# Ten of 22 gate/up pairs of a feed-forward stage as seven half-block products on normalised x

## The chip, the cores and the metric

One core of one Trainium2 chip runs the whole program in one launch. The metric is device microseconds (us) of one execution, and lower is better. TensorE (PE) multiplies a 128x128 weight block (loaded first, by PEld in the profile) with a moving tile of up to 512 columns and adds the result up in PSUM. VectorE (DVE), ScalarE (ACT) and GpSimd (POOL) work on tiles of 128 partitions. SyncE (SP) issues nearly all DMA transfers.

## The reference

Two layers over 512 tokens of width 1024. The four SwiGLU stages, two in each layer, are where the change lies:

```python
def rmsnorm(x, g):
    xf = x.astype(jnp.float32)
    y = xf * lax.rsqrt(jnp.mean(xf * xf, axis=-1, keepdims=True) + RMS_EPS)
    return (y * g.astype(jnp.float32)).astype(x.dtype)

def swiglu(x, w_gate, w_up, w_down):          # 1024 -> 2816 -> 1024
    return (jax.nn.silu(x @ w_gate) * (x @ w_up)) @ w_down

for i in range(DEPTH):                        # DEPTH = 2
    h = h + 0.5 * swiglu(rmsnorm(h, norm_ffn1[i]), ...)
    h = h + mixer_i(rmsnorm(h, norm_mix[i]))  # attention, differs by layer
    h = h + 0.5 * swiglu(rmsnorm(h, norm_ffn2[i]), ...)
    gate = jax.nn.sigmoid(rmsnorm(h, norm_ple[i]) @ w_ple_gate[i])
    h = h + gate * (p[i] @ w_ple_proj[i])
```

All of it is float32. The input embedding p is what "the 256 KB loads of p" below refers to.

## The kernel before, in words

Everything is kept transposed: the feature axis on the partitions, the 512 tokens along the free axis. `h` is eight tiles (chunks) of 128x512.

**Exact products from rounded parts.** PE reads a rounded float32 format (fp32r). Each operand is therefore split in two: `hi`, its rounded copy (ACT, L121), and `lo`, what is left over (DVE, L122: source minus `hi`). `mm3` (L139) then issues three matmuls for each 128x128 weight block: hi·hi, hi·lo and lo·hi (L142 to L144). A *unit* (L129) is 1024 columns of weights: a DMA of 512 KB on SP's queue (L135) into a `wr` tile, then ACT's rounding into `wh` and DVE's low part into `wl`. `mm_unit` multiplies the eight blocks of a unit with the eight chunks of x: 24 matmuls 512 columns wide.

**A feed-forward stage** (`ffn`) has 22 gate/up pairs of 128 hidden features each, then eight output chunks of the down projection. A pair is two units, gate into a bank of PSUM tag `mm`, up into one of tag `sc`, so 48 matmuls. The moving operand is `xg`: h times the gain, split, but not yet divided by the root mean square. That factor, the row `R` (128x512, the same on all partitions), is only known when h is complete and squared, so it is put on afterwards: DVE multiplies the gate bank by R (L236), ACT takes the silu (L237), DVE multiplies the up bank by R (L238), POOL multiplies both (L239), and the product is split for the down projection by ACT and DVE. The 22 products stay in 44 tiles of the pool `act`.

**What sets the order.** The program is written as such a sequence; a scheduler of the framework puts each engine's instructions in a fixed order by the order in which they were written and by when its simulation finds them ready. Code inside `tc.high_priority()` is put ahead. Pools give the buffers: 3 `wr`, 4 `wh`, 4 `wl`, 59 `act`, 8 `tmp`; PSUM banks 3 `mm`, 2 `sc`, 2 `tr`, 1 `ob`. A DMA into a `wr` tile waits until the unit before it in that buffer has been read by ACT and DVE. Each engine, and each DMA queue, takes its instructions strictly in that order. Before the second to fourth feed-forward stages, `rcol` and `R` are made while the first pairs already run on PE; in the first stage the squares are made after the first pair.

**Other stages.** The mixers and the embedding step use the same units. In the V projection of the mixer (L322 to L324) the moving operand is a 256-column slice of the weights, so its matmuls are 256 wide, each with a weight load of its own.

Of the kernel before, what the change touches and what calls it, by code (L numbers as in the profile page):

```python
# [36 lines left out]
class Trunk:
# [52 lines left out]
    def setup(self):  # L90
# [21 lines left out]
        for c in range(KC):  # L112
            self.h[c] = self.hp.tile([P, T], F32, tag="h", name=self.nm("h"))
            nc.sync.dma_start(self.h[c], io["xT"][:, c, :])
            self.norm_split(c)
            if c in (0, 2):
                self.ahead.append(self.unit(io["gu1"][0, 0, c // 2]))
# [99 lines left out]

    def ffn(self, i, which, k_next):
        nc, io = self.nc, self.io
        gu, dn = io[f"gu{which}"], io[f"dn{which}"]  # L220
        xg, a = self.xg, []
        for m in range(NF):
            pgu = []
            for j in range(2):
                u = self.ahead.pop(0) if self.ahead else self.unit(gu[i, m, j])
                p = self.sbank() if j else self.bank()
                self.mm_unit(p, u, xg, True, True)
                pgu.append(p)
                if j == 0 and m == 0 and (i or which == 2):
                    self.rcol  # L230
            if m == 0 and i == 0 and which == 1:
                for c in range(KC):
                    self.norm_square(c)
            R = self.R
            t1, t2 = self.tmp(), self.tmp()
            nc.vector.tensor_tensor(t1, pgu[0], R, op=ALU.mult)  # L236
            nc.scalar.activation(t1, t1, AF.Silu)  # L237
            nc.vector.tensor_tensor(t2, pgu[1], R, op=ALU.mult)  # L238
            nc.gpsimd.tensor_tensor(t2, t1, t2, op=ALU.mult)  # L239
# [822 lines left out]
```

## Time and profile before

| | |
|---|---|
| median of 3 runs | 2126.43 us (2123.27 to 2127.14) |
| the profiled execution | 2126.64 us, of which the span of its instructions 2124.8 us |
| TensorE's granted clock, mean | 1.00 of full speed (0.995) |
| DVE, ACT and POOL busy | 1132.3, 783.8 and 352.3 us |
| POOL's product L239 | 88 instructions, 1309 ns each |
| DMA, mean over the span | 95 GB/s |

How to read it: each engine's busy time is a share of the span, but no stage has the same share. Of interest is the stretch of the pairs, where PE's matmuls follow each other without a gap. Busy time of PE counts matmuls that overlap their neighbours (they are pipelined), so it is the distance between the starts of two matmuls that says what one costs.

### The profile page before, as it was taken

Reading aid. Unit: us, or ns where it says so; the run is one execution under the profiler, and the core shown is the slowest. Engines: PE = TensorE matmul, PEld = TensorE weight load, DVE = VectorE, ACT = ScalarE, POOL = GpSimd, SP = SyncE. Lnnn points to the kernel's source line nnn. Section 1 sums busy time; section 2 is a strip of 40 time slices with the busy share of each in tenths; the row PEclk is TensorE's granted clock in tenths of the full one; section 3 lists DMA queues with packets and bytes.
Section 4 is the critical chain, followed back from the end, with each engine's and each line's share of the span. In section 5 each row is a group of like instructions: output and inputs, shape, how many; then the busy total and the mean of one; then the engine's idle time right before and its main releaser. Section 6 shows DMA issues by size and latency. Waiting matters only on the chain.

```text
span 2124.8 us, 25520 instructions
## 1 busy us (share of the span) xinstructions
PE 2085.4 (98%) x9950; PEld 1734.6 (82%) x9950; DVE 1132.3 (53%) x1793; ACT 783.8 (37%) x1255; POOL 352.3 (17%) x248
## 2 busy tenths in 40 slices
PE   8999999999999999999999999999999999999998
PEld 6888888777787888888888888888888888888886
DVE  6554432699786444543354555333778744553334
ACT  4332222465544333222343233223656533232232
POOL 3111101233211111101111111013222210110111
PEclk9999999999999999999999999999999999999999
DMA  5333333221223233333333322334333223323331
GB/s 171 98 99 99 95 96 98 85 75 56 65 68 92 90 99 99 99 90 96 105 97 99 99 93 93 95 97 124 105 105 102 82 90 99 99 91 96 94 107 60
DMA packets 75385, 202.02 MB, mean 95 GB/s; under 512 B 16896, under 2 KB 24576, under 8 KB 75264
## 3 DMA queue, kind: packets, MB, share of 16 engines
q1 hardware_dynamic: 74976, 200.29, 30.8%
q8 instruction: 78, 1.28, 0.3%
q14 instruction: 43, 0.35, 0.1%
q10 hardware_dynamic: 288, 0.10, 0.0%
HBM read 191.97 MB, written 2.59 MB: 92 GB/s over the span
## 4 chain that ended last, share of the span: by engine, by line
PE 89%; DVE 5%; ACT 2%; issue 1%; POOL 1%; DMA 0%; SPq 0%; DVEq 0%; POOLq 0%; ACTq 0%
PE mm L143 15%; PE mm L144 15%; PE mm L142 15%; PE sc L142 12%; PE sc L143 12%; PE sc L144 12%; PE mm L322 1%; PE mm L323 1%; PE mm L324 1%; PE tr L349 1%; PE ob L359 1%; PE ob L360 1%; PE sc L428 1%; ACT wh L121 1%; DVE act L572 1%
## 5 line engine op out<-in xcount | busy, mean ns | idle before, releaser
L121 ACT ACTIVATE wh<-wr 128x1024 fp32r<-128x1024 f32 (+1 forms) x360 | 374.6, 1042 | 995.0 <-issue 431.1
L122 DVE TENSOR_TENSOR wl<-wr,wh 128x1024 fp32r<-128x1024 f32 (+1 forms) x343 | 510.2, 1488 | 314.1 <-ACT wh L121 313.1
L143 PE MATMUL mm<-act,wh 128*128 128x512 f32 (+1 forms) x1560 | 609.7, 391 | 3.0 <-DVE act L169 2.1
L142 PE MATMUL mm<-act,wh 128*128 128x512 f32 (+1 forms) x1560 | 609.1, 391 | 1.0 <-ACT wh L121 0.6
L144 PE MATMUL mm<-act,wl 128*128 128x512 f32 (+1 forms) x1560 | 608.3, 390 | 0.5 <-DVE wl L122 0.5
L144 PE MATMUL sc<-act,wl 128*128 128x512 f32 (+1 forms) x1138 | 442.5, 389 | 0.8 <-DVE wl L122 0.8
L142 PE MATMUL sc<-act,wh 128*128 128x512 f32 (+1 forms) x1138 | 442.9, 389 | 0.0
L143 PE MATMUL sc<-act,wh 128*128 128x512 f32 (+1 forms) x1138 | 442.5, 389 | 0.0
L143 PEld LDWEIGHTS mm<-act,wh 128*128 128x128 f32 x1560 | 293.4, 188 | 64.4 <-DVE act L169 5.3
L142 PEld LDWEIGHTS mm<-act,wh 128*128 128x128 f32 x1560 | 293.3, 188 | 60.0 <-ACT act L121 1.5
L144 PEld LDWEIGHTS mm<-act,wl 128*128 128x128 f32 x1560 | 293.2, 188 | 58.4 <-DVE wl L122 1.0
L239 POOL TENSOR_TENSOR tmp<-tmp,tmp 128x512 f32<-128x512 f32 x88 | 115.2, 1309 | 818.5 <-DVE tmp L238 783.7
L144 PEld LDWEIGHTS sc<-act,wl 128*128 128x128 f32 x1138 | 213.7, 188 | 45.1 <-DVE wl L122 1.2
L143 PEld LDWEIGHTS sc<-act,wh 128*128 128x128 f32 x1138 | 213.7, 188 | 44.1
L142 PEld LDWEIGHTS sc<-act,wh 128*128 128x128 f32 x1138 | 213.6, 188 | 43.8
L238 DVE TENSOR_TENSOR tmp<-sc,R 128x512 f32<-128x512 f32 x88 | 60.8, 691 | 276.8 <-PE sc L144 276.8
L180 POOL TENSOR_TENSOR ssq<-ssq,tmp 128x512 f32<-128x512 f32 x55 | 90.2, 1639 | 552.6 <-ACT tmp L175 525.7
L236 DVE TENSOR_TENSOR tmp<-mm,R 128x512 f32<-128x512 f32 x88 | 60.8, 691 | 130.4 <-PE mm L144 127.9
L121 ACT ACTIVATE act<-tmp 128x512 fp32r<-128x512 f32 x92 | 58.3, 634 | 117.3 <-POOL tmp L239 116.2
L322 PE MATMUL mm<-wh,act 128*128 128x256 f32 x256 | 74.4, 291 | 0.3 <-DVE act L337 0.3
L323 PE MATMUL mm<-wl,act 128*128 128x256 f32 x256 | 73.9, 289 | 0.0
L324 PE MATMUL mm<-wh,act 128*128 128x256 f32 x256 | 73.8, 288 | 0.0
(142 smaller groups left out, 1621.8 us busy)
## 6 DMA issues: line engine op xcount, KB each, us to landing
wr<-in_gu_dram SPq DMA_DIRECT2D x176, 512.0 KB, 3.5
wr<-in_dn_dram SPq DMA_DIRECT2D x64, 512.0 KB, 3.5
wr<-in_dn_dram SPq DMA_DIRECT2D x32, 384.0 KB, 3.1
wr<-in_qk_ab_dram SPq DMA_DIRECT2D x20, 512.0 KB, 3.5
wr<-in_plg_dram SPq DMA_DIRECT2D x16, 512.0 KB, 3.5
wr<-in_qk_c_dram SPq DMA_DIRECT2D x16, 512.0 KB, 3.7
act<-act SPq DMA_DIRECT2D x40, 128.0 KB, 2.2
wr<-in_v_ab_dram SPq DMA_DIRECT2D x8, 512.0 KB, 3.8
```

What stands on the lines that cost most here:

```text
L121: self.nc.scalar.activation(hi, src, AF.Copy)
L122: (lo_eng or self.nc.vector).tensor_tensor(lo, src, hi.bitcast(F32), op=ALU.subtract)
L142: mm(out, stat[0], mov[0], start=start, stop=False)
L143: mm(out, stat[0], mov[1], start=False, stop=False)
L144: mm(out, stat[1], mov[0], start=False, stop=stop)
L180: eng.tensor_tensor(self.acc, self.acc, sq, op=ALU.add)
L236: nc.vector.tensor_tensor(t1, pgu[0], R, op=ALU.mult)
L238: nc.vector.tensor_tensor(t2, pgu[1], R, op=ALU.mult)
L239: nc.gpsimd.tensor_tensor(t2, t1, t2, op=ALU.mult)
L322: nc.tensor.matmul(ps[b], xh, h, start=first, stop=False, skip_group_check=True)
L323: nc.tensor.matmul(ps[b], xh, l, start=False, stop=False, skip_group_check=True)
L324: nc.tensor.matmul(ps[b], xl, h, start=False, stop=last, skip_group_check=True)
```

## The change: what it does

**The block form.** Of a gate/up pair take the weights as W = [u1 g1; u2 g2] (u up, g gate; 1 and 2 are the two halves of the 1024 input features) and x as halves 1, 2 by features and left, right by tokens. Gate and up for both token halves are then a 2x2 block product. Done directly it needs eight half-block products, each of 4 weight blocks times 256 columns of x. `pair_fast` does it with seven (Strassen's scheme in Winograd's form, in which sums are used again), of which four use sums of weight blocks or sums of x blocks. A half-block product is 4 blocks x 3 matmuls of 256 columns. So 84 matmuls of 256 columns stand where 48 of 512 stood.

**Which pairs.** Of the 22 pairs of each stage the first three (`FRONT`) stay as they were. Pairs 5 to 14 (`FAST`) are done by `pair_fast`, ten in each of four stages. The seven-product form adds blocks of x for different tokens, so x must be normalised first: after pairs 0 and 1, `normal` makes eight normalised chunks y (DVE, L265; each is split again); after pairs 2 and 3, `sums` makes the chunks once more (L276) and from them four sets of sums t of half chunks (L283 to L286), split as well. Pairs 3, 4 and 15 to 21 run on y in the old form with 48 matmuls, without the multiplications by R and without POOL: ACT takes the silu straight from PSUM, DVE multiplies the up bank by it (L259).

**The weights of a fast pair.** The weight tensor is laid out anew in DRAM as [u2 | u1 | g1 g2]. `ra` = [g1 g2] and `rb` = u2 are loaded; `rs` is loaded as [u1 g1] and then a second DMA, on POOL's queue, adds [u2 u1] onto it in place (L298). The transfers are 512, 512, 512 and 256 KB. Two more sums are made by DVE in place in `ra` (L310, L311), after its first split. Four splits (`wa`, `ws`, `wr` and, half as wide, `wb`) feed PE.

**The results.** Seven products end in five half banks: pa (used three times in two halves), pb, pc, pd, pe. They are added up by ACT copies (L330, L336, L342) and DVE additions (L331, L339 to L341, L343), each 256 columns, then silu (L344) and a 512-column product (L345), then the split as before.

**Pools.** `wr` has 4 buffers instead of 3, `act` 57 instead of 59.

```diff
...
+FRONT = 3
+FAST = 5, 15
...
-        self.ap_ = pool("act", 59)
+        self.ap_ = pool("act", 57)
...
-        self.wr = pool("wraw", 3)
+        self.wr = pool("wraw", 4)
...
+    def mm_pair(self, p, u, xs, j):
+
+        for k in range(KC):
+            c = (k + KC // 2 * j) % KC * P
+            self.mm3(p, (u[0][:, c:c + P], u[1][:, c:c + P]), xs[k], k == 0, k == KC - 1)
...
+        t = self.tmp()
+        nc.scalar.activation(t, pgu[0], AF.Silu)
+        nc.vector.tensor_tensor(t, pgu[1], t, op=ALU.mult)
+        return t
...
+    def normal(self, c):
+
+        x = self.tmp()
+        self.nc.vector.scalar_tensor_tensor(x, self.h[c], self.gain[:, self.k, c:c + 1], self.R,
+                                            op0=ALU.mult, op1=ALU.mult)
+        return self.split_chunk(x, self.nc.vector)
+
+    def sums(self, y, c):
...
+        for k in (c, c + KC // 2):
+            x = self.tmp()
+            nc.vector.scalar_tensor_tensor(x, self.h[k], self.gain[:, self.k, k:k + 1], self.R, op0=ALU.mult, op1=ALU.mult)
+            v += [x[:, :H], x[:, H:]]
+        b11, b12, b21, b22 = v
+        s, r = self.tmp(), self.tmp()
+        t1, t2, t3, t4 = s[:, :H], s[:, H:], r[:, :H], r[:, H:]
+        tt = nc.vector.tensor_tensor
+        stt = nc.vector.scalar_tensor_tensor
+        tt(t1, b11, b12, op=ALU.subtract)
+        stt(t2, t1, -1.0, b22, op0=ALU.mult, op1=ALU.subtract)
+        tt(t3, b22, b12, op=ALU.subtract)
+        stt(t4, t2, -1.0, b21, op0=ALU.mult, op1=ALU.subtract)
+        return [self.split_chunk(x, nc.vector) for x in (s, r)]
+
+    def pair_fast(self, w, y, t):
...
+        ra, rs = [self.wr.tile([P, UNIT], F32, tag="wr", name=self.nm("wr")) for _ in range(2)]
+        rb = self.tmp()
+        dma = nc.sync.dma_start
+        dma(rs, w[:, M:M + UNIT])
+        nc.gpsimd.dma_start(rs, w[:, :UNIT], accum_op=ALU.add)
+        dma(ra, w[:, UNIT:])
+        dma(rb, w[:, :M])
...
+        wa, ws = parts(ra), parts(rs)
+        tt(ra[:, :M], ra[:, :M], rs[:, :M], op=ALU.add)
+        tt(ra[:, M:], ra[:, M:], ra[:, :M], op=ALU.add)
+        wr, wb = parts(ra), parts(rb, M)
...
+        def product(out, w, off, xs, x, start, stop):
+            for k in range(half):
+                c = slice(off + k * P, off + (k + 1) * P)
+                mm = nc.tensor.matmul
+                mm(out, w[0][:, c], xs[k][0][:, x], start=start and k == 0, stop=False, skip_group_check=True)
+                mm(out, w[0][:, c], xs[k][1][:, x], start=False, stop=False, skip_group_check=True)
+                mm(out, w[1][:, c], xs[k][0][:, x], start=False, stop=stop and k == half - 1, skip_group_check=True)
...
+        product(pa, wa, 0, y[:half], l, True, False)
+        product(pb, wa, M, y[half:], l, False, False)
+        with self.tc.high_priority():
+            nc.scalar.activation(gt[:, l], pb, AF.Copy)
+            tt(gt[:, l], pa, gt[:, l], op=ALU.add)
+        product(pc, ws, M, t34, l, True, False)
+        product(pd, ws, 0, t12, l, False, True)
+        product(pa, wr, 0, t12, r, False, False)
+        with self.tc.high_priority():
+            nc.scalar.activation(xy[:, l], pa, AF.Copy)
+        product(pe, wb, 0, t34, r, True, True)
+        product(pa, wr, M, y[half:], r, False, True)
+        tt(xy[:, r], pc, xy[:, l], op=ALU.add)
+        tt(up[:, l], pe, xy[:, r], op=ALU.add)
+        tt(up[:, r], pd, xy[:, r], op=ALU.add)
+        nc.scalar.activation(gt[:, r], pa, AF.Copy)
+        tt(gt[:, r], pd, gt[:, r], op=ALU.add)
+        nc.scalar.activation(gt, gt, AF.Silu)
+        nc.vector.scalar_tensor_tensor(gt, up, -1.0, gt, op0=ALU.mult, op1=ALU.mult)
+        return gt
...
             if m < FRONT - 1:
                 n = KC // (FRONT - 1)
                 for c in range(m * n, m * n + n):
                     y[c] = self.normal(c)
             elif FRONT - 1 <= m < FAST[0] - 1:
                 n = KC // 2 // (FAST[0] - FRONT)
                 for c in range((m - FRONT + 1) * n, (m - FRONT + 2) * n):
                     t[c] = self.sums(y, c)
...
```

**How the order of the instructions moves.** PE's program grows by 1440 matmuls, which is 40 pairs times 36. The names below end in a running number; a letter-number like `wh_1333` is one buffer's content. L123 and L124 are the two halves of a split (hi and lo) in the changed kernel, L121 and L122 before.

DVE at the start of the second feed-forward stage, before: the first pairs' multiplications by R and the low parts of the weight units.

```order
L122 TENSOR_TENSOR wl_5976<-wr_5974,wh_5975 128x1024
L236 TENSOR_TENSOR tmp_5861<-mm_5789,R_5854 128x512
L238 TENSOR_TENSOR tmp_5862<-sc_5829,R_5854 128x512
L122 TENSOR_TENSOR act_5868<-tmp_5862,act_5867 128x512
L236 TENSOR_TENSOR tmp_5933<-mm_5877,R_5854 128x512
L122 TENSOR_TENSOR wl_6017<-wr_6015,wh_6016 128x1024
L238 TENSOR_TENSOR tmp_5934<-sc_5908,R_5854 128x512
```

The end of the same entry in the changed kernel, just ahead of the first fast pair. `wl_6900` is the low part of pair 4's second unit, `wl_6944` and `wl_6948` those of the first fast pair's `wa` and `ws`.

```order
L276 SCALAR_TENSOR_TENSOR tmp_6851<-h_174,gain,R_6517 128x512
L124 TENSOR_TENSOR act_6846<-tmp_6836,act_6845 128x512
L283 TENSOR_TENSOR tmp_6853<-tmp_6849 128x256
L285 TENSOR_TENSOR tmp_6854<-tmp_6851,tmp_6849 128x256
L284 SCALAR_TENSOR_TENSOR tmp_6853<-tmp_6853,tmp_6851 128x256
L124 TENSOR_TENSOR wl_6900<-wr_6898,wh_6899 128x1024
L286 SCALAR_TENSOR_TENSOR tmp_6854<-tmp_6853,tmp_6851 128x256
L124 TENSOR_TENSOR act_6860<-tmp_6853,act_6859 128x512
L124 TENSOR_TENSOR wl_6944<-wr_6936,wh_6943 128x1024
L124 TENSOR_TENSOR act_6864<-tmp_6854,act_6863 128x512
L124 TENSOR_TENSOR wl_6948<-wr_6937,wh_6947 128x1024
```

What moved: the work on y and t (eight each of L265 and L276, 16 low parts, 16 half-chunk additions) stands between the weights' low parts, and `wl_6900` comes after nearly all of it.

ACT, before, over two pairs: weight rounding, silu, weight rounding, rounding of the product.

```order
L121 ACTIVATE wh_568<-wr_567 128x1024
L237 ACTIVATE tmp_485<-tmp_485 128x512
L121 ACTIVATE wh_599<-wr_598 128x1024
L121 ACTIVATE act_491<-tmp_486 128x512
L121 ACTIVATE wh_640<-wr_639 128x1024
```

ACT in the changed kernel, across the border between two fast pairs, call them A (tiles 10xx to 11xx) and B (12xx). `wh_1218<-tmp_1199` is the rounding of B's `wb`, `wh_1333` of `wa` of the pair after B, `tmp_1225<-mm_1222` B's copy L330.

```order
L123 ACTIVATE wh_1214<-wr_1197 128x1024
L342 ACTIVATE tmp_1096<-mm_1093 128x256
L344 ACTIVATE tmp_1096<-tmp_1096 128x512
L123 ACTIVATE wh_1218<-tmp_1199 128x512
L123 ACTIVATE wh_1333<-wr_1326 128x1024
L330 ACTIVATE tmp_1225<-mm_1222 128x256
L123 ACTIVATE act_1193<-tmp_1096 128x512
L123 ACTIVATE wh_1337<-wr_1327 128x1024
L336 ACTIVATE tmp_1227<-mm_1222 128x256
L123 ACTIVATE wh_1343<-wr_1326 128x1024
L342 ACTIVATE tmp_1225<-mm_1222 128x256
```

What moved: the copy that the product P6 of a pair needs (L330, then L331 on DVE) stands behind the rounding of `wb`, whose data come by DMA, and here also behind the next `wa`. In every other fast pair or so `wa` comes behind L330 (four of ten pairs in a stage have the order shown).

SP's queue, before:

```order
L135 DMA wr_783<-in_gu_dram 128x1024
L135 DMA wr_814<-in_gu_dram 128x1024
L135 DMA wr_855<-in_gu_dram 128x1024
L135 DMA wr_886<-in_gu_dram 128x1024
L135 DMA wr_927<-in_gu_dram 128x1024
```

SP's queue in the changed kernel: L297 loads `rs`, L299 `ra`, L300 `rb` (a `tmp`).

```order
L297 DMA wr_1069<-in_gu_dram 128x1024
L300 DMA tmp_812<-in_gu_dram 128x512
L299 DMA wr_1068<-in_gu_dram 128x1024
L297 DMA wr_1198<-in_gu_dram 128x1024
L300 DMA tmp_941<-in_gu_dram 128x512
L299 DMA wr_1197<-in_gu_dram 128x1024
L297 DMA wr_1327<-in_gu_dram 128x1024
L300 DMA tmp_1070<-in_gu_dram 128x512
```

What moved: where one kind of transfer stood there are three, and `rb` of a pair (`tmp_1070` belongs to the pair of `wr_1069`) is queued behind `rs` of the pair two later (`wr_1327`). That one waits for its buffer until DVE has made the low part of `ws` from `wr_1069` (`wl_1080`).

## Rows read from the trace of the kernel before

**Rows 1.** The page: busy time of each engine (share of the span) and its instructions.
```profile
PE 2085.4 (98%) x9950; PEld 1734.6 (82%) x9950; DVE 1132.3 (53%) x1793; ACT 783.8 (37%) x1255; POOL 352.3 (17%) x248
```

**Rows 2.** The page: chain of waits that ended last, shares of the span by engine.
```profile
PE 89%; DVE 5%; ACT 2%; issue 1%; POOL 1%; DMA 0%; SPq 0%; DVEq 0%; POOLq 0%; ACTq 0%
```

**Rows 3.** Timeline of PE over one ordinary gate/up pair (start, duration, line, tiles).
```profile
199.86 0.39 PE L142 MATMUL mm<-act,wh 128*128 128x512 f32 x1
...
205.30 0.39 PE L142 MATMUL sc<-act,wh 128*128 128x512 f32 x1
...
210.74 0.39 PE L142 MATMUL mm<-act,wh 128*128 128x512 f32 x1
```

**Rows 4.** Timeline of PE over 41 matmuls of the V projection, 256 columns wide.
```profile
399.76 0.28 PE L323 MATMUL mm<-wl,act 128*128 128x256 f32 x1
...
404.56 0.28 PE L324 MATMUL mm<-wh,act 128*128 128x256 f32 x1
```

**Rows 5.** Groups by line and shape: weight loads of the V projection (count, busy us, mean ns).
```profile
L322 PEld LDWEIGHTS mm<-wh,act 128*128 128x128 f32 x256 | 50.2, 196 | 1.1 <-DVE act L337 0.9
```

**Rows 6.** Timeline of DVE over the same ordinary pair.
```profile
200.06 0.69 DVE L238 TENSOR_TENSOR tmp<-sc,R 128x512 f32<-128x512 f32 x1 [3.30 <-PE sc L144]
200.97 2.32 DVE L122 TENSOR_TENSOR wl<-wr,wh 128x1024 fp32r<-128x1024 f32 x1 [0.23 <-ACT wh L121]
203.21 0.68 DVE L122 TENSOR_TENSOR act<-tmp,act 128x512 fp32r<-128x512 f32 x1
206.41 1.23 DVE L122 TENSOR_TENSOR wl<-wr,wh 128x1024 fp32r<-128x1024 f32 x1 [0.22 <-ACT wh L121]
```

**Rows 7.** Timeline of ACT over the same pair.
```profile
205.32 1.06 ACT L121 ACTIVATE wh<-wr 128x1024 fp32r<-128x1024 f32 x1 [2.44 <-PE mm L143]
206.28 0.61 ACT L237 ACTIVATE tmp<-tmp 128x512 f32<-128x512 f32 x1
213.12 0.63 ACT L121 ACTIVATE act<-tmp 128x512 fp32r<-128x512 f32 x1 [1.30 <-POOL tmp L239]
```

**Rows 8.** Timeline of POOL over the same pair.
```profile
200.92 1.29 POOL L239 TENSOR_TENSOR tmp<-tmp,tmp 128x512 f32<-128x512 f32 x1 [9.59 <-DVE tmp L238]
```

**Rows 9.** Timeline of DVE around the start of the second feed-forward stage.
```profile
679.59 1.22 DVE L122 TENSOR_TENSOR wl<-wr,wh 128x1024 fp32r<-128x1024 f32 x1 [0.23 <-ACT wh L121]
680.73 0.75 DVE L169 SCALAR_TENSOR_TENSOR act<-h,gain,act 128x512 fp32r<-128x512 f32 x1
...
698.00 0.68 DVE L236 TENSOR_TENSOR tmp<-mm,R 128x512 f32<-128x512 f32 x1
698.60 0.68 DVE L238 TENSOR_TENSOR tmp<-sc,R 128x512 f32<-128x512 f32 x1
...
707.28 0.69 DVE L238 TENSOR_TENSOR tmp<-sc,R 128x512 f32<-128x512 f32 x1 [3.30 <-PE sc L144]
```

**Rows 10.** Timeline of DVE in the first feed-forward stage.
```profile
28.31 0.68 DVE L238 TENSOR_TENSOR tmp<-sc,R 128x512 f32<-128x512 f32 x1
...
36.86 0.69 DVE L238 TENSOR_TENSOR tmp<-sc,R 128x512 f32<-128x512 f32 x1 [2.46 <-PE sc L144]
```

**Rows 11.** Groups by line and shape: DVE, a 256-column addition of two SBUF tiles.
```profile
L890 DVE TENSOR_TENSOR h<-h,tmp 128x256 f32<-128x256 f32 x8 | 3.4, 423 | 0.2
```

**Rows 12.** Groups by line and shape: ACT, the 256-column copy from PSUM.
```profile
L121 ACT ACTIVATE tmp<-tr 128x256 fp32r<-128x256 f32 x32 | 12.2, 382 | 18.6 <-PE tr L349 18.2
```

**Rows 13.** The gate/up weight tensor's DMAs: issue ns, then us to landing.
```profile
L135 SPq DMA_DIRECT2D wr<-in_gu_dram x176: 327/328/561, 1.2 to 1899.8; - x176
DMA to landing us min/median/max: 3.3/3.5/7.1
```

**Rows 14.** The 256 KB loads of p, queued among 512 KB weight loads: us to landing.
```profile
DMA to landing us min/median/max: 3.8/4.1/4.4
```

**Rows 15.** Stretches: busy us of PE, PEld, DVE, ACT, POOL (instructions); clock; DMA share, GB/s.
```profile
7.00:13.00 6.00, 4.13 (x13) 2.09 (x14) 5.27 (x5) 5.79 (x10) 4.72 (x3) 1.00 1.04 403
200.00:222.00 22.00, 22.00 (x99) 18.22 (x98) 11.23 (x11) 6.79 (x9) 2.58 (x2) 1.00 0.29 95
```

More of the change, by code (lines that the diff above doesn't have):

```diff
@@ L116, in setup @@
             if c in (0, 2):
[L117 removed]
+                self.ahead.append(self.unit(io["gu1"][0, 0, :, (1 - c // 2) * UNIT:(2 - c // 2) * UNIT]))
     def split(self, src, hi, lo, lo_eng=None):
@@ L215, in R, with pair_front @@
         return self.rt
+    def pair_front(self, w, m, first):
+        nc = self.nc
+        pgu = []
+        for j in range(2):
+            u = self.ahead.pop(0) if self.ahead else self.unit(w[:, (1 - j) * UNIT:(2 - j) * UNIT])
+            p = self.sbank() if j else self.bank()
+            self.mm_pair(p, u, self.xg, j)
+            pgu.append(p)
+            if j == 0 and m == 0 and not first:
+                self.rcol
+        if m == 0 and first:
+            for c in range(KC):
+                self.norm_square(c)
+        R = self.R
+        t1, t2 = self.tmp(), self.tmp()
+        nc.vector.tensor_tensor(t1, pgu[0], R, op=ALU.mult)
+        nc.scalar.activation(t1, t1, AF.Silu)
+        nc.vector.tensor_tensor(t2, pgu[1], R, op=ALU.mult)
+        nc.gpsimd.tensor_tensor(t2, t1, t2, op=ALU.mult)
+        return t2
@@ new lines, in mm_pair, with pair @@
+    def mm_pair(self, p, u, xs, j):
+        for k in range(KC):
+            c = (k + KC // 2 * j) % KC * P
+            self.mm3(p, (u[0][:, c:c + P], u[1][:, c:c + P]), xs[k], k == 0, k == KC - 1)
+    def pair(self, w, y):
+        nc = self.nc
+        pgu = []
+        for j in range(2):
+            u = self.unit(w[:, (1 - j) * UNIT:(2 - j) * UNIT])
+            p = self.sbank() if j else self.bank()
+            self.mm_pair(p, u, y, j)
+            pgu.append(p)
+        t = self.tmp()
+        nc.scalar.activation(t, pgu[0], AF.Silu)
+        nc.vector.tensor_tensor(t, pgu[1], t, op=ALU.mult)
+        return t
@@ L220, in ffn @@
         gu, dn = io[f"gu{which}"], io[f"dn{which}"]
-        xg, a = self.xg, []
+        first = i == 0 and which == 1
+        a, y, t = [], [None] * KC, [None] * (KC // 2)
         for m in range(NF):
[L223 to L239, printed above, removed]
+            if m < FRONT:
+                r = self.pair_front(gu[i, m], m, first)
+            elif FAST[0] <= m < FAST[1]:
+                r = self.pair_fast(gu[i, m], y, t)
+            else:
+                r = self.pair(gu[i, m], y)
             ah, al = self.act(F32R), self.act(F32R)
-            self.split(t2, ah, al)
+            self.split(r, ah, al)
             a.append((ah, al))
+            if m < FRONT - 1:
+                n = KC // (FRONT - 1)
+                for c in range(m * n, m * n + n):
+                    y[c] = self.normal(c)
+            elif FRONT - 1 <= m < FAST[0] - 1:
+                n = KC // 2 // (FAST[0] - FRONT)
+                for c in range((m - FRONT + 1) * n, (m - FRONT + 2) * n):
+                    t[c] = self.sums(y, c)
         self.begin_norm(k_next)
```

20 lines of the change are left out of this document (19 added, 1 removed).

## The prediction, made before the changed kernel had run

> **What bounds the kernel now.** I read the page first: PE is busy for 98% of the span with 9950 matmuls [rows 1], and the chain that ended last runs over PE for 89% of its length, over DVE for 5% [rows 2]. So time is won by PE doing less, as long as nobody makes it wait. What a matmul costs is read from the starts on the PE timeline, since busy time counts overlaps twice. An ordinary pair takes 210.74 − 199.86 = 10.88 us for 48 matmuls of 512 columns, 226.7 ns each [rows 3]. In the V projection 40 steps of 256 columns take 4.80 us, 120 ns each [rows 4]. The other engines' timelines over the same pair show what they do in it: DVE two low parts of the weights, two products with R and a low part of the result, ACT three roundings and a silu [rows 6, 7]. The table of stretches sums it: in 22.00 us DVE is busy for 11.23 and ACT for 6.79 [rows 15], so both have half the time free or more. The profiled execution took 2126.64 us, the median is 2126.43, 0.2 lower; I work from 2126.64.
>
> **Matmuls.** A fast pair is 84 × 120 ns = 10.08 us instead of 10.88, so 0.80 us less, 40 times: **−32 us**. Seven products for eight would be worth an eighth, 1.36 us; 0.56 is lost because the narrow matmul costs 120 ns and not half of 226.7. Both widths were measured without waits, so this term is firm if weight loads hide. A load lasts 196 ns where one starts every 120 ns [rows 5, 4], so loads overlap and do hide there. The Trainium skill, "Perfetto Trace Analysis", Identifying the Most-Contended Engine, calls weight-load busy time, and not matmul busy time, a good measure of how near TensorE is to its limit; by that rule 84 loads for 48 speak against the change. Rows 4 and 5 do not bear it out; it is a rival below.
>
> **Entry of each stage.** DVE now makes y and t while the first five pairs run. How far apart two of its instructions start is about 0.08 less than what they last: 1.14 for a 1024-column low part (679.59 to 680.73), 0.60 for a 512-column product from PSUM [rows 9], 0.67 for one with a scalar, 0.33 for a 256-column addition (423 ns long [rows 11]) and 0.40 with a scalar. A low part that meets a POOL product takes 2.32 instead of 1.23 [rows 6, 8], 1.09 more. In the second stage the first R product ran at 698.60 [rows 9], and from 699.2 on DVE has, before PE can end pair 4: 16 scalar products (10.7), 18 low parts of 512 (10.8), 4 of 1024 (4.6), 5 evacuations (3.0), 15 of the 16 half-chunk additions (5.5), and three meetings with POOL (3.3). Sum 37.9, so 737.1. PE ended pair 1 at 707.1, just ahead of the second R product on its up bank (707.28). Pairs 2 and 3 and the first unit of pair 4 follow, 2.5 × 10.88, and the low part of the second unit, which stands behind all that work in DVE's line, is wanted 0.45 later by the third matmul: 734.75. PE waits 2.4 us. In the first stage, whose R products come at 28.31 and 36.86 [rows 10], the same sum gives 28.9 + 37.9 = 66.8 against 36.7 + 27.65 = 64.35, 2.5 us. 3 × 2.4 + 2.5 = **+10 us**. Bounds: 0, if no POOL product meets a low part, and 20, if two or three more low parts a stage are met.
>
> **Steady state of fast pairs.** DVE's own work in one is four low parts (3 × 1.14 + 0.60), the two weight sums L310 and L311 (1.2), five half-width additions (1.7), L345 (0.67) and the product's low part (0.60), 8.2 us. Some 0.15 for each of six steps that must see the end of the one before makes 9.1, and waits for ACT's roundings (1.06 each, where DVE has nothing else ready) about 9.9, an estimate from the order, against PE's 10.08. ACT has roundings of 3 × 1.06 + 0.63, three 382-ns copies [rows 12], a silu of 0.61 and a rounding of 0.63 [rows 7]: 6.2 us. POOL's product, 1.29 us [rows 8], goes. So neither engine becomes the bound, but DVE has hardly any reserve, and order decides.
>
> The critical order is this. Time 0 is P6, the fifth product, of pair A; the half bank it fills in pair B must be emptied by L330 (ACT) and L331 (DVE) by 10.08. ACT rounds `ws`(B) from 0.2 on, DVE ends its low part at 2.5; that frees the raw buffer for `rs` of pair D, two later. SP issues this one (0.33 us a transfer [rows 13]) and then `rb`(B), which was queued behind it, at 3.0. `rb` is 256 KB behind a 512 KB transfer, like the loads of p: 3.8 to 4.4 us, median 4.1, which I take [rows 14]. It lands at 7.1, and ACT rounds `wb` until 7.7. Without the transfer it could start at 6.8. Where `wa` of the next pair stands before L330 (four pairs of ten), it follows to 8.7, L330 to 9.0, and DVE, busy with the low part of `wa` until 10.0, ends L331 at 10.4: 0.35 us late, equal to the landing time less 3.75. In the other order a landing of up to 4.4 to 4.85 costs nothing. 16 pairs × 0.35 = **+5.6 us**; 2 at a landing of 3.8, 10 at 4.4, 15 at 4.6, 27 at 5.0, where the pairs of the other order wait as well.
>
> **The adding DMA.** No row shows one. Below it cannot be cheaper than an ordinary 512 KB load, 3.5 us; the slowest landing of a gate/up load was 7.1 [rows 13], and I take that as the upper end, since the bytes are read and added in place. Neither end counts: `rs` of a pair is issued about when `ws` of the pair two before it is done, and needed two pairs, 20.16 us, later; less 2.6 for the split and 4.1 for the plain load, 13.5 are left. It costs 0 up to there. The Trainium skill, "DMA: Bandwidth & Descriptors", Anatomy of one DMA — SWDGE (gpsimd) path, gives 2.0 us plus bytes by 436e3 for a transfer from this queue, by which 512 KB take an estimated 3.2 us and the term stays nothing; no run here shows it. The load on the DMA engines is 1.75 MB in 10.08 us, 174 GB/s instead of 95; at the start of the program 403 GB/s went through [rows 15], so bandwidth does not bind.
>
> **Nothing else.** The pairs on y that are not fast lose L236 and POOL's product but have PE's 10.88 as before: 0 us, hidden by PE. The pool `act` with two tiles less can hold back only the last low parts before the down projection, when PE has eight chunks to do: 0. Mixers, embedding and down projection keep their order.
>
> **Sum.** −32 + 10 + 5.6 = −16.4, and 2126.64 − 16.4 = **2110 us**.
>
> **The rivals.**
> 1. *Nothing waits.* The entry's 2.4 us and the 0.35 us of a pair both vanish: −32, 2095. For it: before, DVE and ACT wait and not PE. Against: 37.9 us of counted work in the entry.
> 2. *`rb` lands late and P6 waits.* It ends on the other side. SP holds `rb` behind an `rs` that waits for a buffer, and each microsecond of landing beyond 4.85 is lost in nearly all 40 pairs. At 4.85 us the whole change is worth nothing (32 − 10 = 22 us of lateness); at 5.0 it gives 2126.64 − 32 + 10 + 27 = 2132. For it: three transfers of 512 KB now stand near the 256 KB one. Against: the loads of p did not pass 4.4 [rows 14]. From 4.6 to 5.2: 2120 to 2140.
> 3. *DVE is slowed by POOL's transfer.* If preparing the adding DMA costs DVE in each fast pair what one POOL product costs a low part, 1.09 us [rows 6], the loop is 9.9 + 1.09 = 10.97, 0.09 over the old pair: 40 × 0.09 + 10 = +13.6, so 2140. The row shows the meeting for a product; for a DMA nothing does.
> 4. *The adding DMA is slow.* It decides from 13.5 us. At 20 us two pairs would take 6.5 more, 3.2 each: −32 + 10 + 130 gives 2235. Against: 7.1 is the slowest seen.
> 5. *Weight loads bound PE.* If loads of 196 ns [rows 5] did not overlap, 84 of them would make a pair 16.5 us: 40 × 5.6 = +224, so 2351. Against: one started every 120 ns [rows 4]. It is what the rule of the Trainium skill's page "Perfetto Trace Analysis", named above, would make of this change.
>
> That the change does not do what it says is excluded: PE has 1440 more matmuls, 40 × 36.
>
> **How the numbers follow.** My forecast, a small loss in each entry and in the pairs of one order, gets 0.45, with a range of its own of 2102 to 2120 (entry 5 to 15, lateness 2 to 10). Rival 1 gets 0.10, rival 2 0.23, rival 3 0.13, rival 4 0.07, rival 5 0.02. What a measurement of this kernel can tell from no change is about 0.2%, 4.3 us. Faster: 0.45 + 0.10 + 0.3 × 0.23 = 0.62. Same: 0.35 × 0.23 = 0.08. Slower: the other 0.35 × 0.23 and rivals 3, 4 and 5, 0.30. The range runs from rival 1 to rivals 2 and 3, 2095 to 2140. Rivals 4 and 5 lie outside, and rivals 1 and 3, which stand on its edges, with half their chance: 0.09 + 0.12, which is the 2 in 10.
>
> **What would show it.** Right: starts of matmuls in fast pairs 120 ns apart, fast pairs 10.1 to 10.5 us from first to first matmul; a wait of PE of 2 to 4 us at the second unit of pair 4, released by DVE's L124; alternating gaps of some tenths before the fifth product, released by L331. Wrong: a gap before the fifth product in all fast pairs (rival 2, with `rb` landing over 4.85 us; or rival 3, with DVE's low parts over 2 us beside L298), a gap at the third product released by ACT's rounding of `ws` (rival 4), or 190 ns between matmuls (rival 5). The forecast falls if the time is under 2102 or over 2120.

## The result, and the profile after

The changed kernel takes 2135.06 us (median of 4 runs, 2130.49 to 2137.89), beside 2126.21 before: a ratio of 1.0043, 95% interval 1.0027 to 1.0058. It is 9 us slower where 16 us faster were forecast. The profiled execution has a span of 2133.1 us, 8.3 more than before. The page's busy line and the first line of its chain, which answer to [rows 1] and [rows 2]:

```profile
PE 2064.9 (97%) x11390; PEld 1781.0 (83%) x11390; DVE 1289.2 (60%) x2269; ACT 916.2 (43%) x1519; POOL 291.6 (14%) x212
PE 76%; DVE 12%; ACT 3%; DMA 3%; issue 2%; POOL 2%; SPq 0%; POOLq 0%; DVEq 0%; ACTq 0%
```

PE is busy for 20.5 us less, and 1440 matmuls more are there. But the chain runs over PE for 76% instead of 89% of its length, and DVE and DMA have 15% where they had 5%. PE now waits. The view of waits says for whom (engine, line and tile that waited, what for, us in total, times, longest); its first two rows:

```profile
PE mm L321 <- DVE tmp L331: 15.6, 17, 1.4
PE sc L146 <- DVE wl L124: 12.4, 4, 3.7
```

The first row is the fifth product (P6 in the prediction) waiting until L331 has read its half bank. The second is the low part of pair 4's second unit, once in each stage. Both places were forecast; the sizes were 5.6 and 10.

The matmuls themselves went as forecast. On the PE timeline 11 steps within a fast pair take 1.32 us, 120 ns each:

```profile
94.48 0.28 PE L321 MATMUL mm<-act,wh 128*128 128x256 f32 x1
...
95.80 0.28 PE L323 MATMUL mm<-act,wl 128*128 128x256 f32 x1
```

From the start of each fast pair to the start of the next (worked out from that timeline) a pair without a wait takes 10.08 us. In the second stage:

```
pair            5      6      7      8      9     10     11     12     13     14
change       20.27  10.08  11.34  10.31  11.75  10.08  11.57  10.08  11.33  10.29
```

Pair 5 begins with four matmuls that run before pair 4 is done, and 22 matmuls of pair 4 follow them; without a wait it would show 10.08 + 22 x 0.2267 = 15.07. That makes an account of the whole change, from one execution of each kernel:

| term | forecast | measured |
|---|---|---|
| matmuls, 40 x (10.08 − 10.88) | −32 | −32.0 |
| entries (pairs 5: 78.9 in four stages, 60.3 without a wait) | +10 | +18.6 |
| the other 36 fast pairs over 10.08 | +5.6 | +20.8 |
| start of the program | 0 | +1.5 |
| everything else | 0 | −0.7 |
| sum | −16.4 | +8.2, of 8.3 in the span |

**Why P6 waits.** SP, ACT and DVE around pair 9 of the second stage. P6 of pair 8 started at 783.8, so P6 of pair 9 was due at 793.9; it started at 795.5.

```profile
783.79 0.39 PE L321 MATMUL mm<-act,wh 128*128 128x256 f32 x1
...
795.54 0.39 PE L321 MATMUL mm<-act,wh 128*128 128x256 f32 x1 [1.42 <-DVE tmp L331]
```

```profile
787.56 0.33 SPq L297 DMA_DIRECT2D wr<-in_gu_dram  x1
787.94 0.43 SPq L300 DMA_DIRECT2D tmp<-in_gu_dram  x1
```

```profile
792.31 0.63 ACT L123 ACTIVATE wh<-tmp 128x512 fp32r<-128x512 f32 x1 [0.40 <-DMA tmp<-in_gu_dram]
792.85 1.04 ACT L123 ACTIVATE wh<-wr 128x1024 fp32r<-128x1024 f32 x1
793.80 0.36 ACT L330 ACTIVATE tmp<-mm 128x256 f32<-128x256 f32 x1
```

```profile
784.45 1.23 DVE L124 TENSOR_TENSOR wl<-wr,wh 128x1024 fp32r<-128x1024 f32 x1
785.71 0.69 DVE L310 TENSOR_TENSOR wr<-wr,wr 128x512 f32<-128x512 f32 x1
786.32 1.22 DVE L124 TENSOR_TENSOR wl<-wr,wh 128x1024 fp32r<-128x1024 f32 x1
...
793.92 1.23 DVE L124 TENSOR_TENSOR wl<-wr,wh 128x1024 fp32r<-128x1024 f32 x1 [0.26 <-ACT wh L123]
795.07 0.42 DVE L331 TENSOR_TENSOR tmp<-mm,tmp 128x256 f32<-128x256 f32 x1
```

Read it from the top of DVE: `wa`'s low part, the sum L310, then `ws`'s low part, which ends at 787.54, 3.7 us after P6 of the pair before. Only then does SP issue `rs` of a later pair (L297), and behind it `rb` (L300) at 787.94. `rb` lands at 792.3, 4.35 us later, and ACT was idle for it. Its rounding, the next `wa` and L330 follow, and DVE makes the next `wa`'s low part before L331. This is the forecast's chain link by link, started 1.2 us later.

The same holds in all 16 pairs of this order, which are pairs 9, 11, 13 and 14 of each stage (worked out from the traces of SP, ACT, DVE and PE). In each of them L331 ends 3.2 us after `rb` has landed; the forecast had 3.3. Pairs 14 follow a pair of their own order: there `rb` was issued 2.8 us after P6 of the pair before, and three of the four lost 0.2 us, the fourth 0.8. Pairs 9, 11 and 13 follow a pair of the other order: `rb` was issued 3.0 to 4.2 us after that P6, and they lost 0.6 to 1.7 us. The 16 pairs lose 16.7 of the 20.8 us; most of the rest is in pairs 7, where `rb` was issued up to 4.3 us after P6.

**Why the entry is late.** DVE and POOL in the second stage, where PE waits from 736.8 to 740.0:

```profile
714.27 0.69 DVE L124 TENSOR_TENSOR act<-tmp,act 128x512 fp32r<-128x512 f32 x1 [1.85 <-ACT act L123]
...
725.96 0.69 DVE L124 TENSOR_TENSOR act<-tmp,act 128x512 fp32r<-128x512 f32 x1 [2.13 <-ACT act L123]
...
738.73 1.22 DVE L124 TENSOR_TENSOR wl<-wr,wh 128x1024 fp32r<-128x1024 f32 x1
```

```profile
711.08 0.93 POOL L298 DMA_DIRECT2D wr<-in_gu_dram  x1 [8.52 <-DVE tmp L265]
711.74 1.83 POOL L239 TENSOR_TENSOR tmp<-tmp,tmp 128x512 f32<-128x512 f32 x1
723.06 0.88 POOL L298 DMA_DIRECT2D wr<-in_gu_dram  x1 [9.49 <-DVE tmp L285]
723.67 1.60 POOL L239 TENSOR_TENSOR tmp<-tmp,tmp 128x512 f32<-128x512 f32 x1
```

```profile
713.61 1.68 ACT L123 ACTIVATE act<-tmp 128x512 fp32r<-128x512 f32 x3 [3.97 <-POOL tmp L239]
725.30 1.15 ACT L123 ACTIVATE act<-tmp 128x512 fp32r<-128x512 f32 x2 [4.83 <-POOL tmp L239]
```

DVE stood still twice, 4.0 us in all, for the rounding of a front pair's product on ACT, which waited for POOL's L239. POOL had the product's last input from DVE's L238 at 709.8 and 720.8, but each time an adding DMA (L298) stood ahead of it in POOL's queue. That DMA adds onto a plain load, which landed at 710.3 and 722.5, and so could not start before. The product itself took 1.6 to 1.8 us, 1.29 in [rows 8].

**The clock.** In the second, third and fourth stages the wait (3.2, 3.5 and 3.7 us) was followed by a lower clock. Stretches (us, busy us of PE, PEld, DVE, ACT, POOL with instructions, granted clock, DMA share, GB/s): one behind the wait of the second stage, then before, in and after the wait of the third:

```profile
740.30:743.70 3.40, 3.40 (x9) 2.65 (x8) 3.40 (x5) 0.63 (x1) 0.00 (x0) 0.50 0.53 154
...
1150.00:1156.00 6.00, 6.00 (x28) 4.99 (x27) 6.00 (x13) 3.37 (x5) 0.00 (x0) 1.00 0.00 1
1156.80:1160.60 3.80, 0.32 (x3) 0.12 (x1) 3.80 (x8) 1.58 (x3) 0.00 (x0) 0.94 0.26 69
1161.00:1163.40 2.40, 2.40 (x7) 1.82 (x7) 2.40 (x4) 0.61 (x1) 0.00 (x0) 0.50 0.67 179
1164.00:1170.00 6.00, 6.00 (x40) 5.43 (x39) 4.40 (x7) 2.38 (x4) 0.66 (x1) 1.00 0.31 87
```

In the first and the fourth of these rows the granted clock is 0.50, the lower of its two levels (1.2 GHz), and a 512-column matmul starts every 0.43 us instead of 0.227. After the wait of 1.9 us in the first stage the clock stayed at 1.00. Of the 18.6 us the four waits are 12.4. In the first stage, without the lower clock, the entry cost 0.44 more than its wait, for the restart behind it; four times that is 1.8, and the 4.4 that are left go with the lower clock.

### The profile page after: what moved, and what is told of

It is laid out like the page before. It is cut to its first block, busy times and chain, and to the rows that moved or that the text cites. A ratio compares the mean times of both kernels' runs of the same rounds, so it can differ in the third digit from the quotient of the medians.

```text
span 2133.1 us, 29295 instructions
## 1 busy us (share of the span) xinstructions
PE 2064.9 (97%) x11390; PEld 1781.0 (83%) x11390; DVE 1289.2 (60%) x2269; ACT 916.2 (43%) x1519; POOL 291.6 (14%) x212
## 4 chain that ended last, share of the span: by engine, by line
PE 76%; DVE 12%; ACT 3%; DMA 3%; issue 2%; POOL 2%; SPq 0%; POOLq 0%; DVEq 0%; ACTq 0%
PE mm L145 10%; PE mm L146 10%; PE mm L144 10%; PE sc L146 7%; PE sc L144 7%; PE sc L145 7%; PE mm L321 3%; PE mm L323 3%; PE mm L322 3%; DVE wl L124 3%; DVE act L124 2%; PE sc L321 1%; PE sc L322 1%; PE sc L323 1%; DMA wr<-in_gu_dram 1%
## 5 line engine op out<-in xcount | busy, mean ns | idle before, releaser
L123 ACT ACTIVATE wh<-wr 128x1024 fp32r<-128x1024 f32 (+1 forms) x400 | 415.0, 1041 | 784.8 <-PE mm L145 286.3
L124 DVE TENSOR_TENSOR wl<-wr,wh 128x1024 fp32r<-128x1024 f32 (+1 forms) x383 | 468.7, 1224 | 385.6 <-ACT wh L123 382.6
L145 PE MATMUL mm<-act,wh 128*128 128x512 f32 x1240 | 485.0, 391 | 2.6 <-DVE act L171 1.6
L144 PE MATMUL mm<-act,wh 128*128 128x512 f32 x1240 | 484.7, 391 | 1.1 <-ACT wh L123 0.8
L146 PE MATMUL mm<-act,wl 128*128 128x512 f32 x1240 | 483.8, 390 | 0.5 <-DVE wl L124 0.5
L146 PE MATMUL sc<-act,wl 128*128 128x512 f32 x818 | 320.3, 392 | 12.4 <-DVE wl L124 12.4
L144 PE MATMUL sc<-act,wh 128*128 128x512 f32 x818 | 320.5, 392 | 0.0
L145 PE MATMUL sc<-act,wh 128*128 128x512 f32 x818 | 320.1, 391 | 0.0
L145 PEld LDWEIGHTS mm<-act,wh 128*128 128x128 f32 x1240 | 233.1, 188 | 51.8 <-DVE act L171 5.1
L144 PEld LDWEIGHTS mm<-act,wh 128*128 128x128 f32 x1240 | 233.1, 188 | 47.7 <-ACT wh L123 1.6
L146 PEld LDWEIGHTS mm<-act,wl 128*128 128x128 f32 x1240 | 233.1, 188 | 46.0 <-DVE wl L124 1.0
L321 PE MATMUL mm<-act,wh 128*128 128x256 f32 x640 | 183.7, 287 | 15.6 <-DVE tmp L331 15.6
L146 PEld LDWEIGHTS sc<-act,wl 128*128 128x128 f32 x818 | 154.8, 189 | 45.7 <-DVE wl L124 13.6
L145 PEld LDWEIGHTS sc<-act,wh 128*128 128x128 f32 x818 | 154.7, 189 | 32.2
L323 PE MATMUL mm<-act,wl 128*128 128x256 f32 x640 | 181.1, 283 | 0.0
L144 PEld LDWEIGHTS sc<-act,wh 128*128 128x128 f32 x818 | 154.8, 189 | 31.5
L322 PE MATMUL mm<-act,wh 128*128 128x256 f32 x640 | 181.0, 283 | 0.0
L321 PEld LDWEIGHTS mm<-act,wh 128*128 128x128 f32 x640 | 122.6, 192 | 20.3 <-DVE tmp L331 19.6
L123 ACT ACTIVATE act<-tmp 128x512 fp32r<-128x512 f32 x156 | 95.4, 625 | 75.3 <-POOL tmp L239 38.8
L322 PEld LDWEIGHTS mm<-act,wh 128*128 128x128 f32 x640 | 122.7, 192 | 0.2
L323 PEld LDWEIGHTS mm<-act,wl 128*128 128x128 f32 x640 | 122.7, 192 | 0.2
```

Of the source, the lines that this page charges most:

```text
L123: self.nc.scalar.activation(hi, src, AF.Copy)
L124: (lo_eng or self.nc.vector).tensor_tensor(lo, src, hi.bitcast(F32), op=ALU.subtract)
L144: mm(out, stat[0], mov[0], start=start, stop=False)
L145: mm(out, stat[0], mov[1], start=False, stop=False)
L146: mm(out, stat[1], mov[0], start=False, stop=stop)
L321: mm(out, w[0][:, c], xs[k][0][:, x], start=start and k == 0, stop=False, skip_group_check=True)
```

## The experiments

Three theories stood against each other. **A**: two queues are to blame, SP's, where `rb` stands behind an `rs` that waits, and POOL's, where products stand behind adding DMAs; the two are independent. **B**: DVE has no reserve, and the waits will show up elsewhere if they are mended. **C**: the adding DMA itself slows DVE or the other transfers.

**e1: `rb` in a buffer of its own.**

```diff
-        rb = self.tmp()
+        rb = self.tp.tile([P, T], F32, tag="rb", name=self.nm("rb"), bufs=1)
```

> Edit: rb gets one buffer of its own (a tag rb with one buffer in the pool tmp) instead of a turn of the eight tmp tiles. On SP rb of a pair then stands ahead of rs of the pair two later, and on ACT and DVE the split of wb comes before the silu in every fast pair. Theory A (rb is late because it is queued behind an rs that waits for the low part of ws): the gaps before the fifth product, 21 us in all four stages of the changed kernel, shrink to under 5, time 2114 to 2120. Rival B (DVE has no reserve in a fast pair, the order only says where that shows): the gaps move to another product but keep their sum, 2130 to 2137. Rival C (the adding DMA makes DVE or the other transfers slow): the same, 2130 to 2137, with low parts over 1.23 us beside the adding DMA.

2115.0 us, ratio 0.9948 (0.9933 to 0.9963). The wait for L331 is gone from the table, the wait of the entries stays (one of the five, 0.8 us, lies at the start of the program):

```profile
PE sc L146 <- DVE wl L124: 12.1, 5, 3.4
```

Each of the 36 pairs takes 10.13 us, 1.8 us over 10.08 in all instead of 20.8. `rb` is now issued 3.9 us ahead of the fifth product of the pair before (785.1 in the second stage), not 4.1 behind it:

```profile
781.19 0.33 SPq L300 DMA_DIRECT2D rb<-in_gu_dram  x1
```

Its transfer did not become faster: 4.4 us median instead of 4.3. How often ACT's rounding waited for it (us, times), in the change and in e1:

```profile
  ACT wh L123: 34.1, 34
DMA to landing us min/median/max: 2.7/4.3/5.4
```

```profile
  ACT wh L123: 1.3, 2
DMA to landing us min/median/max: 3.4/4.4/6.7
```

The next `wa` stands ahead of L330 in every pair here, so it is the start of `rb` that counts, and not its duration or that order. Theory A holds here; B and C, which expected the sum to stay, fall.

**e2: fast pairs 7 to 16 instead of 5 to 14.**

```diff
-FAST = 5, 15
+FAST = 7, 17
```

> Edit: the ten fast pairs are 7 to 16 instead of 5 to 14, and the four sums of t are made one a pair after pairs 2 to 5 instead of two a pair. Theory A (DVE is late at the entry because all of y and t must be made before pair 4 ends): the waits of PE for the low part in the entry (2.2, 3.3, 3.7 and 3.9 us, with the restarts and the half clock after them 17) go to under 2 in all, the gaps before the fifth product stay at 15 to 22, time 2115 to 2122. Rival B (the entry is late by DVE's whole work, wherever it is put): PE waits the same 15 to 17 two pairs later, 2133 to 2137.

The four sums are then made one a pair instead of two. 2112.93 us, ratio 0.9937 (0.9922 to 0.9952). The entry wait for L124 is no longer in the table; the first row is now

```profile
PE mm L321 <- DVE tmp L331: 10.6, 18, 1.3
```

and the fast pairs lose 17.0 us over 40 x 10.08, as expected. The time is 2 us under the expected range.

**e3: both.** The two edits together.

> Edit: both of the edits before. Theory A: the two gains add, 2097 to 2104, that is 2126 less 32 and plus 2 to 9. Rival B: one wait takes the place of the other, 2115 to 2137.

2097.55 us, ratio 0.9865 (0.985 to 0.9879), within the range of theory A: the two gains add. Neither row is left, and 40 fast pairs lose 2.3 us.

**e4: no fast pairs.**

```diff
-FAST = 5, 15
+FAST = 5, 5
```

> Edit: no fast pair at all (FAST = 5, 5), pairs 3 to 21 on y with 48 matmuls; y and t are made as in the change, t is not used. Theory A (the entry's price is that of y and t alone): 2126 plus 12 to 19, 2138 to 2145, with the same wait of PE at the second unit of pair 4. Rival (the entry is late because of the first fast pair's larger weight work, which shares the line): under 6 us over before, 2126 to 2132.

2133.97 us, ratio 1.0034 (1.002 to 1.0049): 8 us over before, between the two. The same place waits, but less than half as long:

```profile
PE sc L146 <- DVE wl L124: 5.3, 4, 1.5
```

Making y and t explains less than half of the entry's waits. The rest comes with the fast pairs, and I had not said how. The POOL rows above suggested it; the next two runs test it.

**e5: without the adding DMA.**

```diff
-        nc.gpsimd.dma_start(rs, w[:, :UNIT], accum_op=ALU.add)
```

> Edit: the adding DMA (L298) is left out, so rs holds [u1 g1] alone and the sums of weights are not formed; every other instruction stays. Theory A (in the entry two adding DMAs stand in POOL's queue ahead of the products of pairs 1 and 2 and wait for their plain loads; DVE then waits for those products): the waits of PE in the entry fall from 12.4 to about 5 us, as in the kernel without fast pairs, and the gaps before the fifth product stay at 15 to 22; time 2123 to 2130. Rival C (the adding DMA slows the 256 KB transfer or DVE): the gaps before the fifth product fall under 8 us, 2110 to 2118. Rival D (it costs nothing at all): 2132 to 2137.

2123.4 us (10 runs, 2120.8 to 2128.5), ratio 0.999 (0.998 to 0.9999), in A's range and 12 below the change. The kernel leaves the sums of weights out. The profiled execution was the slowest of the ten. Its first two rows:

```profile
PE mm L320 <- DVE tmp L330: 15.6, 15, 1.9
PE sc L146 <- DVE wl L124: 7.9, 5, 1.9
```

The entry falls from 18.6 to 10.4 us (pairs 5: 70.7), and the fast pairs lose 21.3, as with it; the 256 KB transfer still takes 4.3 us (median). So the adding DMA does not slow the steady state (C falls), and its cost lies in the entry. The trace accounts for 8 of the 12 us; where the other executions, all faster, gained the rest was not seen.

**e6: the front pairs' product on DVE.**

```diff
-        nc.gpsimd.tensor_tensor(t2, t1, t2, op=ALU.mult)
+        nc.vector.tensor_tensor(t2, t1, t2, op=ALU.mult)
```

> Edit: the product of the three front pairs (L239) on DVE instead of POOL, so no product of POOL is behind an adding DMA, and DVE has 3 x 0.6 us more work in an entry. Theory A (DVE waits 1.9 and 2.1 us in the second stage's entry for products that are late on POOL): entry waits 12.4 to 4 to 9 us, time 2125 to 2131. Rival (DVE is short of time there by its own work): entry waits 14 to 22, time 2136 to 2144.

2121.01 us, ratio 0.9976 (0.9967 to 0.9986): DVE has more to do, and the kernel is 14 us faster than the change, 4 below A's range. The entry wait:

```profile
PE sc L146 <- DVE wl L124: 4.9, 5, 1.0
```

Pairs 5 take 66.2 us, 5.9 over no wait. The two adding DMAs stand in POOL's queue as before, now with nothing behind them:

```profile
707.59 0.93 POOL L298 DMA_DIRECT2D wr<-in_gu_dram  x1 [16.12 <-DVE tmp L265]
719.45 0.87 POOL L298 DMA_DIRECT2D wr<-in_gu_dram  x1 [10.94 <-DVE tmp L239]
```

The waits in the entries are 1.0 us each and the clock stays at 1.00 after them, so that part of the 18.6 goes too.

**e7: the split of `ws` first.** No buffer is added; two splits change places.

```diff
-        wa, ws = parts(ra), parts(rs)
+        ws, wa = parts(rs), parts(ra)
```

> Edit: in pair_fast the split of ws is written ahead of that of wa, nothing else; no buffer is added. On ACT and DVE ws of a pair then comes before wa and before L310, and on SP rb stands ahead of the rs two pairs later. Theory A (the low part of ws ends 1.2 us later than I had taken, since wa's low part and L310 stand before it, and rb starts only then): gaps before the fifth product under 5 us, time 2113 to 2120. Rival (DVE's reserve is used up, wa is now what comes late): PE waits before the first product instead, 2128 to 2140.

2117.66 us, ratio 0.9957 (0.994 to 0.9974). L331 is gone from the table, the 36 pairs lose 1.8 us, and the waits of the entry are nearly as they were:

```profile
PE sc L146 <- DVE wl L124: 12.6, 5, 3.4
```

Pairs 5 take 81.2 us, 2.3 more than in the change: the granted clock was 0.50 after all four waits here, after three there. In this kernel SP has `rb` ahead of the `rs` two pairs later. Its transfers take longer than in the change and cost nothing:

```profile
  ACT wh L123: 0.2, 1
DMA to landing us min/median/max: 2.6/5.3/9.1
```

**e8: eleven fast pairs.** e1 with `FAST = 7, 18`.

> Edit: rb in its own buffer and FAST = 7, 18, eleven fast pairs a stage. Theory A: each further fast pair is worth 10.88 less 10.13, four of them 3.0 us: 2093 to 2096. Rival (the 32 tiles of y and t, held one pair longer, keep the splits of results waiting for act tiles, and the down projection starts late): 2097 to 2106.

2096.29 us (2092.59 to 2097.34), ratio 0.9857 (0.9843 to 0.9872), on the border between the two expectations. All 44 pairs but one take 10.12 to 10.13 us in the trace, but the profiled span is only 0.4 under that of e3. Matmul by matmul, the four stretches of fast pairs gain 3.0 us more on the kernel before than those of e3, as theory A has it, and no down projection starts later. Some 2 us are lost again in the mixers: 0.9 of them near 390 us, where the granted clock was 0.50 from 388.7 to 392.1 and 1.00 in e3, and as much near 1480 us, for a reason that stays open.

**e9: both failed steps mended, fast pairs where they were.** The edits of e6 and e7 together.

> Edit: the split of ws ahead of that of wa, and the front product on DVE; fast pairs stay 5 to 14, pools as in the change. Theory A (the two steps that failed are rb's start and the products behind the adding DMAs, and they are independent): 2126.2 less 32, plus 4 for the entry, 2 for the fifth product's restart and 1.5 at the start of the program: 2101 to 2106. Rival (mending one makes the other worse, DVE being full): 2108 to 2120.

2103.57 us (2102.37 to 2103.95), ratio 0.9897 (0.9883 to 0.9912), within A's range. The wait for L331 is gone, and of the entry there is left

```profile
PE sc L146 <- DVE wl L124: 4.3, 5, 1.0
```

Its account: −32.0 + 5.9 + 2.1 + 1.5 = −22.5, and the span is 2100.6 − 2124.8 = −24.2. The difference lies between the first and the second stage, where this kernel needs 1.8 us less than the one before; the cause stays open. So the time fits the expected sum in part by luck, since the sum had 4 for the entry.

**e10: the best.** e9 with `FAST = 7, 18`.

> Edit: as in the run before, with fast pairs 7 to 17. Theory A: nothing of the entry is left and a fourth of the eleven-pair gain comes on top as with rb in its own buffer: 2093 to 2097. Rival (DVE's three more products bring the entry wait back): 2098 to 2104.

2096.25 us (2095.81 to 2096.44), ratio 0.9864 (0.9847 to 0.988): the fastest with e8, 30 us below the kernel before, without an extra buffer.

**e11: `rb` from ACT's queue.**

```diff
-        dma(rb, w[:, :M])
+        nc.scalar.dma_start(rb, w[:, :M])
```

> Edit: the same rb transfer from ACT's queue, where it stands behind the rounding of wr and so starts some 2 us later than in the change; the ACT order has L330 ahead of the next wa in every pair. Theory A (what decides is when rb starts): wb cannot be rounded before 10.2 us after the fifth product, L331 ends at about 12.3 instead of 10.08, so every fast pair takes 12 to 12.6 us, 80 to 100 us more in all: 2190 to 2220. Rival (SP's queue was the trouble, not the start of rb): gaps under 5 us, 2112 to 2122.

2122.64 us (10 runs, 2117.19 to 2127.7), ratio 0.9987 (0.9977 to 0.9997): neither. My number was off by some 70 us because the start I took was wrong. On ACT the transfer stands behind the rounding of `wr`, but is issued while that rounding starts:

```profile
813.40 1.06 ACT L123 ACTIVATE wh<-wr 128x1024 fp32r<-128x1024 f32 x1 [0.98 <-PE ob L322]
813.41 0.33 ACTq L300 DMA_DIRECT2D tmp<-in_gu_dram  x1
...
817.29 0.63 ACT L123 ACTIVATE wh<-tmp 128x512 fp32r<-128x512 f32 x1 [0.57 <-DMA tmp<-in_gu_dram]
...
818.35 0.36 ACT L330 ACTIVATE tmp<-mm 128x256 f32<-128x256 f32 x1
```

That is 3.0 us after P6 of the pair before (810.4), just what the prediction had for SP. With that start, and L330 ahead of the next `wa` in all pairs but the last of a stage, most pairs take 10.08 us; the 36 lose 6.4 us, in a few pairs. The transfer is shorter too:

```profile
DMA to landing us min/median/max: 2.6/3.4/6.4
```

In the order with L330 ahead, transfers of up to 4.7 us cost at most 0.1 us a pair, and the three of 5.8 to 6.4 us cost 1.2 to 1.8; the prediction had let up to 4.4 to 4.85 us cost nothing there. The order that failed, with the next `wa` ahead, this run does not test: only pairs 14 have it.

## Why the prediction was wrong, step by step

**Matmuls: right.** 120 ns, 10.08 us, −32 us. Rival 5 (weight loads bind) is out: 11390 loads were busy for 1781.0 us, and 256-column matmuls still started every 120 ns. On the Trainium skill's measure ("Perfetto Trace Analysis", Identifying the Most-Contended Engine) the load on TensorE rose, from 82% to 83% of the span, and 85% in e10. These traces do not agree with the rule as the prediction used it: the share went up in the slower kernel and in the faster one.

**The critical order of a fast pair: the step that failed.** The prediction said that DVE ends the low part of `ws`(B) at 2.5 and SP issues `rb` at 3.0. In pair 9 of the second stage it ended at 3.7, since `wa`'s low part and L310 stand before it when the pair before had the other order; I had timed a pair as if each followed one of its own kind. Twelve of the 16 pairs do not; in these `rb` was issued 3.6 us after P6 on average. The transfer took 4.35 in that pair instead of 4.1 [rows 14]. Both were added to a chain that had no reserve: 0.35 + 1.2 + 0.25 = 1.8 us by that sum, 1.7 in that pair, and the term became 20.8 instead of 5.6. The chain behind the landing was right, 3.2 us for 3.3, and so was the start where a pair follows its own kind (pairs 14). Runs e1 and e7 remove the late start in two different ways, and the pairs lose 19 us less in each. Rival 2 is what happened (2120 to 2140), by its place and its sign. But its reason, a landing beyond 4.85 us, was not the cause: the median was 4.3, 5.4 the most, and the issue came late; nor did it touch nearly all 40 pairs, since 14 of the 36 take 10.08. That its range holds the time is in part luck, since the entry's 8.6 went into it.

**Entry: right place, too small (+10, measured +18.6), for reasons that the sum did not have.** The waits themselves were 12.4. DVE's work was counted well: from 700.66 to the end of the low part at 739.95 are 39.3 us, 37.9 were forecast. But of the 3.3 us for meetings with POOL only about 1 came as a meeting (four L265 in a row took 3.77 us from 700.66 on, where three steps of 0.67 and a last one of 0.75 make 2.8). The other 4.0 were waits for products behind adding DMAs. I had priced the DMA, and not what stood behind it in POOL's queue. e5 takes 8 us off the entry by leaving that DMA out, e6 12.7 by taking the products from POOL. The rest of the miss is what comes behind a wait: 1.8 us for the four restarts and 4.4 beside the lower clock, which followed the three longest waits. The sum had priced the waits alone.

**The adding DMA: its price was in the bounds, and hidden.** 6.6 us median, between 3.5 and 7.1, though the slowest took 8.0:

```profile
wr<-in_gu_dram POOLq DMA_DIRECT2D x40, 512.0 KB, 6.6
```

The estimate from the Trainium skill ("DMA: Bandwidth & Descriptors", Anatomy of one DMA — SWDGE (gpsimd) path), 3.2 us, does not hold for an adding transfer here; the measured figure decides. Rival 4 is out (13.5 us were free), and so is rival 3 (whose 9.9 + 1.09 is 10.99 and not 10.97, which changes little): around the adding DMA at 792.26 DVE's low parts kept their 0.69 and 1.23 us, and e5 gains nothing in the fast pairs. Rival 1 came near in e3, after two repairs.

**What was taken as nothing.** The start of the program cost 1.5 us, of which 0.9 is POOL's `rcol` (1.95 us instead of 1.02). Why it is slower was not tried. The other zeros held to some tenths: what lies between two stages differs from before by 0.4 us at most.

**The chances.** Slower had 0.30, faster 0.62. The likeliest case stood on a chain that was late by 0.35 us to begin with, and whose first time was put together from an order and not from a row. Neither miss alone would have made the change slower: 15.2 us in the pairs, 8.6 in the entries and 1.5 at the start of the program together turn −16.4 into +8.9.

## What to carry to other kernels

Where a loop's reserve is a few tenths of a microsecond, time the chain through two iterations, since the one before may have another order; and if the chain has a transfer in it, look first at what stands ahead of its issue in the queue, because an earlier start is often free (e7 only swaps two names, and gains 17 us). Before an operation is put on an idle queue, look at what will stand behind it while it waits: an adding DMA that costs its engine 0.86 us held up two products, and with them DVE and PE. And where a stage's new form needs operands made first, start it later if the number of iterations allows: e2 moves the same ten pairs by two and gains 22 us, 18 of them in the entry.

## What the runs showed of the hardware that was not expected

- TensorE's granted clock fell to 0.50 after the entry's waits of 3.2, 3.5 and 3.7 us in the change, and not after the one of 1.9. After a wait of 1.9 us in the first stage it fell in e5 and e7 and stayed at 1.00 in the change and in e1, so here the length of the wait alone does not decide.
- A DMA on ACT's queue was issued 0.01 us after the start of the ACT instruction ahead of it (813.40 and 813.41), not after its end.
- A product whose half bank is read just in time can cost a little without a wait in the table. In e1 L331 ends 10.04 us after the fifth product of the pair before, the step behind the fifth product's first matmul takes 0.18 us instead of 0.12, and a pair takes 10.13 us; so it is in e3, e7 and e10. In most pairs of e11 and in 14 of 36 of the change it is 10.08.
- Some kernels spread more than others: e5, e6 and e11 by 7.7, 6.4 and 10.5 us in nine or ten runs, the kernel before by 3.7 in 18, e10 by 0.6 in four. That the transfer on the path does it is not shown: e2, with its late `rb`, spread by 1.7 in four runs, e7 without by 4.0.
